# One decode step of a hybrid model: weights loaded from ScalarE's queue, and the recurrence's outer products as matrix products

## The chip, the cores and the metric

The kernel runs on one core of one Trainium2 chip. The metric is the device time of one execution in microseconds; the kernel before took 1142.68 us (median of 3 runs, 1138.63 to 1144.46). A core has five engines that run side by side, each with its own queue of instructions that it works through in order: TensorE (PE in the profile; its weight loads are PEld), VectorE (DVE), ScalarE (ACT), GpSimd (POOL) and SyncE (SP). SP does nothing here but issue DMAs; ACT and POOL issue DMAs too. All DMAs run on the core's 16 DMA engines.

## What is computed

One inference step of one layer for two kinds of tokens at once: a prompt of 512 tokens, and 8 sample requests of one token each with 4096 past tokens. The width is 1024.

```
h  = rmsnorm(x) ; z = h @ w_in              # q, f, v, gate of the recurrence | q, k, v of the attention
S  = f * S + outer(k, v) ; o_hg = q @ S     # gated linear recurrence, 4 heads of 128 x 128
o_da = (softmax(s1) - lam * softmax(s2)) @ v    # differential attention, 4 heads; samples over 32 pages of 128 keys
x  = x + concat(norm(o_hg) * silu(gate), norm(o_da)) @ w_out
x  = x + cross_attention(rmsnorm(x), memory) @ w_mo
x  = x + (silu(h @ w_gate) * (h @ w_up)) @ w_down
```

For the samples the recurrence is one step: the stored state S of each request and head (128 x 128) is scaled by f along its rows and gets the outer product of k and v added; the new state is an output, and q @ S goes on. The samples' attention reads 256 pages of keys and 256 of values, 256 KB each, 134 MB in all; they are the larger part of what is read.

## The kernel before

**Prompt.** Every weight matrix is streamed once. The list `plan` (lines 583 to 608) cuts it into 138 loads of 256 rows by up to 512 columns (512 KB), in the order in which they are used: w_in, the memory's w_mk and w_mv, w_out, w_mq, w_mo, then gate, up and down of the feed-forward part. `load_weights` (613) brings each into a tile `raw`, of which there are three (RAW, later up to six more from the ring `stream`); each load waits until an earlier raw has been used up. ScalarE casts 128 x 512 of it to a rounded `hi` (`round_weights`, 655), VectorE makes the remainder `lo` = raw - hi (`remainders`, 669), with three buffers each (HILO), and `block` (696) makes three products per tile, hi x hi, hi x lo and lo x hi, so that fp32 weights keep their precision; these are the matmuls `mm`.

**Samples.** The same raw tiles are used for the 8 sample rows (`follow`, 2083: sacc, sgm, sgu, sdn). Pages of keys and values come into the ring `stream` (six buffers of two pages) by `gather` (942), issued by SP; `score_keys` (991) multiplies them with the placed queries (`ks`), `sample_softmax` (1024) follows, then `sum_values` (1109, `pv`). Between them stands the prompt's own attention (`da_head`, 1168: sc, pr, pt, oda).

**The samples' recurrence** (`sample_recurrence`, 1474). After the gates, the rows v of all samples (`svq`, 128 x 128: head and sample on the partitions) are written to DRAM (`spill`, 569, the tile `vd`). Then for each of the 8 samples b: GpSimd loads the state `st` and, with `load_row` (575), the four heads' rows of v, copied onto all 128 partitions (`kv`); ScalarE scales each head's part by the column k, `skT[:, h, b]`, which makes the outer product; VectorE adds it to the scaled state, head by head (line 1509); GpSimd stores the state, and TensorE multiplies it with the placed query (`so`).

```
    def load_row(dst, d, b):
        pool.dma_start(dst.rearrange("p (g c) -> p g c", g=4), d[b].partition_broadcast(P))
```

**The order of the work.** Every part is a generator, and `Weave` (312) runs them against a model of the engines' clocks (`Clock`, 134): at each step it takes the stream of the best rank whose data should be there by the model's time of TensorE. What it emits goes to each engine's queue in that order, and the engines run it in order, held by semaphores. A DMA's price in the model stands in `note` (line 248): 0.56 us of the shared issue, and 0.56 us of SP's own time or 0.06 us of ScalarE's. PSUM has 8 banks; the classes mm, at and pv share them (4, 4 and 2 at most).

The weights and the pages are all issued by SP (lines 646 and 952), in one order.

Of the kernel before, what the change touches and what calls it, by code (L numbers as in the profile page):

```python
# [12 lines left out]
F32 = mybir.dt.float32  # L13
# [7 lines left out]
P = 128  # L21
# [4 lines left out]
NB = 8  # L26
# [107 lines left out]
class Clock:  # L134
# [99 lines left out]
    def note(self, e, op, ins):  # L234
        i = ins.ins
        outs = [y.bass_ap for y in i.outs if hasattr(y, "bass_ap")]
        srcs = [y.bass_ap for y in i.ins if hasattr(y, "bass_ap")]
        mine = lambda aps: [a.tensor.name for a in aps if self.tc.is_my_tile(a.tensor)]
        ws, rs = mine(outs), mine(srcs)
        start = self.free[e]  # L240
        at = "dma" if op == "dma_start" else e
        for t in ws + rs:
            w, by = self.wrote.get(t, (0.0, ""))
            if by != at or at == "dma" and t in rs:
                start = max(start, w + self.LATE.get(by, 0.0))
        for t in ws if at != "dma" else ():
            start = max(start, self.used.get(t, 0.0))
        if op == "dma_start":
            if e == "pool":
                self.free[e] = start + 1.0  # L250
            else:
                start = max(start, self.free["issue"])
                self.free["issue"] = start + 0.56
                self.free[e] = start + (0.56 if e == "sp" else 0.06)
            begin = max(self.free["dma"], start + (1.1 if e != "pool" else 2.0))
            a = outs[0] if ws else srcs[0]
            end = self.free["dma"] = begin + 4 * int(np.prod(a.shape)) / 0.37e6
            done = end + 0.93
            e = "dma"
        else:  # L260
            aps = outs + (srcs if e != "pe" else [])
            n = max(int(np.prod(a.shape[1:])) for a in aps)
            holds = self.shared(e, op, outs, srcs)
            if holds:
                for a, b in self.port["pool" if e == "dve" else "dve"]:
                    if a <= start < b:
                        start = b
            done = end = start + self._cost(e, op, outs[0].shape, [a.dtype for a in outs + srcs], n)
            if e == "pe":
                form = "narrow" if outs[0].shape[0] < P else "wide" if F32R in [a.dtype for a in srcs] else "exact"  # L270
                done = end = end + CHANGE.get((self.form, form), 0.0)
                self.form = form
                self.records += 2 if form == "wide" or op == "transpose" else 4
                if self.records >= 256:
                    self.records -= 256
                    done = end = self.fetched = max(end, self.fetched + FETCH)
                tick, rows = int(start / TICK), srcs[0].shape[0] / P
                if self.columns.get(tick - 1, 0) < FULL:
                    done = end = end + (end - start)
                self.columns[tick] = self.columns.get(tick, 0) + n * rows * (1 if F32R in [a.dtype for a in srcs] or op == "transpose" else 2)  # L280
            self.free[e] = end
            self.span = (start, end)
            if holds:
                self.port[e].append((start, end))
        for t in ws:
            self.wrote[t] = (done, e)
            self.mark = max(self.mark, done + self.LATE.get(e, 0.0))
        self.noted += 1
        for t in ws + rs:
            self.used[t] = max(self.used.get(t, 0.0), end)  # L290
            if t in self.banks:
                self.banks[t][1] = self.noted
# [86 lines left out]
def decode_step(ctx: ExitStack, tc: tile.TileContext, io: dict):  # L379
# [186 lines left out]
        use(pt[:, :P].rearrange("p (g b) -> p g b", b=32))  # L566
        at_give()

    def spill(q, name):

        d = dp.tile([P, P], F32, name=name)
        pool.dma_start(d, q)
        return d.rearrange("(g b) c -> b g c", b=32)

    def load_row(dst, d, b):

        pool.dma_start(dst.rearrange("p (g c) -> p g c", g=4), d[b].partition_broadcast(P))


    sizes = [512] * (DFF // 512)  # L580
    sizes.insert(SMALL, DFF % 512)
# [35 lines left out]
    def load_weights():  # L617
        live = deque()

        def home():  # L620

            while live and live[0][0] < min(done["lo"] // 2, done["seen"]):
                live.popleft()
            rings = [t for _, t in live]
            if rings.count("raw") < RAW:
                return "raw", RAW, wp
            if "passed" in S and rings.count("stream") < KBUFS:
                return "stream", KBUFS, kp

        for r, (w, k, c0, ncol, _) in enumerate(plan):  # L630
            yield home
            tag, bufs, pool_ = home()
            live.append((r, tag))
            yield clock.next(tag, bufs)
            raw = ring(pool_, [P, 2, 512], tag, bufs, "raw")[:, :, :ncol]
            src = w[k * P : (k + 2) * P, c0 : c0 + ncol].rearrange("(k p) c -> p k c", p=P)
            if r == 0:
                load_x(0)
                for i in range(2):
                    sync.dma_start(raw[:, i, :], src[:, i, :])  # L640
                load_x(1)
            else:
                if r < 4:
                    load_x(2 * r)
                    load_x(2 * r + 1)
                sync.dma_start(raw, src)
            raws[r] = raw
            if r == CON:
                sync.dma_start(con, io["consts"])
                sync.dma_start(lamv, io["lamv"].partition_broadcast(P))  # L650
                sync.dma_start(ptab, io["ptab"])
            if r == 3:
                sync.dma_start(ropep, io["ropep"])
# [820 lines left out]
    def sample_recurrence(sqT, sfT, svq, sgT):  # L1474
        skT = keep([P, 4, 8], "skT")
        lb3 = lb.unsqueeze(2).to_broadcast([P, 4, 8])
        om3 = omlb.unsqueeze(2).to_broadcast([P, 4, 8])
        sig = rsmall([P, 4, 8], "sig")
        yield from sigmoid(sig, skT, sfT)
        dve.scalar_tensor_tensor(skT, skT, BIG, sig, op0=ALU.min, op1=ALU.mult)  # L1480
        dve.tensor_tensor(skT, skT, om3, op=ALU.mult)
        dve.tensor_tensor(sig, sig, om3, op=ALU.mult)
        dve.tensor_tensor(sfT, sig, lb3, op=ALU.add)
        yield
        sig2 = rsmall([P, 4, 8], "sig")
        yield from sigmoid(sig2, sig2, sgT)
        dve.tensor_mul(sgT, sgT, sig2)
        vd = spill(svq, "vd")
        yield from room(2)
        for b in range(NB):  # L1490
            st = slot("st")
            pool.dma_start(st, io["state"][b])
            kv = slot("kv")
            load_row(kv, vd, b)
            yield
            for h in range(HEADS):
                sl = slice(h * P, (h + 1) * P)
                act.activation(kv[:, sl], kv[:, sl], AF.Copy, scale=skT[:, h, b : b + 1])
            qm = quadt("qm", (P, 4, 32))
            dve.tensor_tensor(  # L1500
                qm,
                sqT[:, :, b : b + 1].to_broadcast([P, 4, 32]),
                ohrow[:, 7 - b : 39 - b].unsqueeze(1).to_broadcast([P, 4, 32]),
                op=ALU.mult,
            )
            yield
            for h in range(HEADS):
                sl = slice(h * P, (h + 1) * P)
                dve.scalar_tensor_tensor(
                    st[:, sl], st[:, sl], sfT[:, h, b : b + 1], kv[:, sl], op0=ALU.mult, op1=ALU.add  # L1510
                )
            yield
            pool.dma_start(io["hg_sample"][b], st)
            yield from at_room()
            po = att("so")
            for h in range(HEADS):
                mm(po[32 * h : 32 * h + 32, :P], qm[:, h, :], st[:, h * P : (h + 1) * P], True, True)
            yield (po,)
            if b == 0:
                dve.tensor_copy(ohg, po[:, :P])  # L1520
            else:
                dve.tensor_add(ohg, ohg, po[:, :P])
            at_give()
        give(2)
        yield
        pool.memset(mixT_s[:, :4, :], 0.0)
        yield from s_headnorm(
            ohg,
            lambda oht: dve.scalar_tensor_tensor(
                mixT_s[:, :4, :8], oht[:, :, :8], hgcol, sgT, op0=ALU.mult, op1=ALU.mult  # L1530
            ),
        )
        S["hgo"] = True
# [1079 lines left out]
```

## Time and profile before

| | |
|---|---|
| median of 3 runs | 1142.68 us (1138.63 to 1144.46) |
| the profiled execution's own time | 1134.85 us |
| its span, first to last instruction | 1133.1 us |
| TensorE busy | 1072.3 us, 95% |
| VectorE, ScalarE, GpSimd busy | 546.1, 428.3, 70.4 us |
| mean granted TensorE clock | 0.974 |
| DMA read, written | 269.35 MB, 8.88 MB |

The profile is that of one execution. Of a group of instructions it gives the busy time, the mean duration in ns, and the idle time of the engine just before them with what ended it. Names are the program's: `ks<-cache_k,qst` writes the tile ks and reads cache_k and qst. Almost all instructions are recorded by one helper and so have one line, L305; go by the names. The ends of matmuls are modelled, so a busy TensorE may hide short waits. fp32 products are recorded as two instructions each, those of rounded operands as one.

### The profile page before, as it was taken

What the parts mean: (1) busy time and instruction counts of PE and PEld (TensorE: products, weight loads), DVE (VectorE), ACT (ScalarE), POOL (GpSimd) and SP (SyncE); (2) the same over time, 40 slices, a digit from 0 to 9 for tenths busy, and PEclk for the clock granted to TensorE, in tenths of its full rate; (3) what the DMA queues carried; (4) which work ended last, traced back from release to release, by engine and by line L of the source; (5) the groups of instructions that cost most, each with busy time, mean ns of one, the idle gap of its engine ahead of it and who ended that gap; (6) DMA issues with size and microseconds to landing.
All of it is one profiled execution on the core that took longest, in us unless ns stands there. A gap on an engine that the chain in (4) does not pass through costs nothing.

```text
span 1133.1 us, 23098 instructions
## 1 busy us (share of the span) xinstructions
PE 1072.3 (95%) x8846; PEld 777.3 (69%) x8846; DVE 546.1 (48%) x1126; ACT 428.3 (38%) x915; POOL 70.4 (6%) x97
## 2 busy tenths in 40 slices
PE   8999799987987889899999999999999999999997
PEld 6777587865665557466666666776577677777776
DVE  6743777534654654444443443453343333443535
ACT  6413443436454556333444332341232221222333
POOL 0000010213101110000300000000000000000002
PEclk9999899988998989999999999999999999999999
DMA  7979665998999995999998799579978982234102
GB/s 255 352 242 324 206 215 174 291 253 259 319 308 278 274 304 169 309 329 332 319 338 285 241 325 343 201 244 359 344 266 291 351 305 75 63 89 129 38 1 75
DMA packets 143376, 279.75 MB, mean 247 GB/s; under 512 B 15281, under 2 KB 20529, under 8 KB 143266
## 3 DMA queue, kind: packets, MB, share of 16 engines
q1 hardware_dynamic: 137970, 264.13, 67.8%
q0 software_dynamic: 4064, 13.05, 6.1%
q8 instruction: 69, 1.13, 0.4%
q10 hardware_dynamic: 1232, 1.11, 0.3%
q14 instruction: 41, 0.34, 0.1%
HBM read 269.35 MB, written 8.88 MB: 246 GB/s over the span
## 4 chain that ended last, share of the span: by engine, by line
PE 81%; DMA 10%; DVE 3%; issue 3%; ACT 1%; SPq 1%; POOL 0%; DVEq 0%; POOLq 0%; ACTq 0%
PE mm L305 56%; DMA cache_k<-cache_k 6%; PE pv L305 5%; PE ks L305 4%; PE sgu L305 2%; PE cs L305 2%; PE sdn L305 1%; DMA kv<-vd 1%; PE ss L305 1%; PE co L305 1%; PE sgm L305 1%; PE pd L305 1%; PE sacc L305 1%; PE oda L305 1%; PE cpv L305 1%
## 5 line engine op out<-in xcount | busy, mean ns | idle before, releaser
L305 DVE TENSOR_TENSOR lo<-raw,hi 128x512 fp32r<-128x512 f32 (+1 forms) x260 | 176.6, 681 | 434.2 <-ACT hi L305 406.1
L305 PE MATMUL mm<-sh,hi 128*128 128x512 f32 (+1 forms) x832 | 339.8, 408 | 4.2 <-ACT sh L305 3.9
L305 ACT CAST hi<-raw 128x512 fp32r<-128x512 f32 (+1 forms) x260 | 157.5, 607 | 490.5 <-PE mm L305 443.3
L305 PE MATMUL mm<-sl,hi 128*128 128x512 f32 (+1 forms) x832 | 324.1, 390 | 0.8 <-DVE sl L305 0.8
L305 PE MATMUL mm<-sh,lo 128*128 128x512 f32 (+1 forms) x832 | 323.0, 388 | 0.0
L305 PEld LDWEIGHTS mm<-sh,hi 128*128 128x128 f32 x832 | 157.2, 189 | 78.6 <-issue 39.0
L305 PEld LDWEIGHTS mm<-sh,lo 128*128 128x128 f32 x832 | 157.5, 189 | 34.0 <-DVE lo L305 0.4
L305 PEld LDWEIGHTS mm<-sl,hi 128*128 128x128 f32 x832 | 157.8, 190 | 28.9 <-DVE sl L305 1.4
L305 PE MATMUL ks<-cache_k,qst 128*32 128x128 f32 x2048 | 72.3, 285 | 16.1 <-DMA cache_k<-cache_k 16.0
L305 PEld LDWEIGHTS ks<-cache_k,qst 128*32 128x32 f32 x2048 | 57.6, 114 | 32.7 <-DMA cache_k<-cache_k 24.0
L305 PE MATMUL pv<-cache_v,wt 128*32 128x512 f32 x512 | 63.4, 608 | 0.0
L305 PE MATMUL mm<-hi,sh 128*128 128x512 f32 x128 | 54.5, 426 | 0.0
L305 PE MATMUL mm<-lo,sh 128*128 128x512 f32 x128 | 50.5, 395 | 0.0
L305 PE MATMUL mm<-hi,sl 128*128 128x512 f32 x128 | 50.5, 394 | 0.0
L305 DVE TENSOR_TENSOR res<-mm,res 128x512 f32<-128x512 f32 (+1 forms) x68 | 42.2, 652 | 9.2 <-PE mm L305 9.2
L305 PEld LDWEIGHTS pv<-cache_v,wt 128*32 128x32 f32 x512 | 14.5, 110 | 31.1 <-issue 22.1
L305 DVE SCALAR_TENSOR_TENSOR lo<-raw,par,hi 128x512 fp32r<-128x512 f32 x16 | 13.2, 826 | 35.1 <-ACT hi L305 35.1
L305 PEld LDWEIGHTS mm<-hi,sh 128*128 128x128 f32 x128 | 24.3, 190 | 7.9 <-issue 3.1
L305 PE MATMUL mm<-hi,mh 128*128 128x512 f32 x64 | 28.5, 446 | 0.9 <-ACT hi L305 0.9
L305 PEld LDWEIGHTS mm<-hi,sl 128*128 128x128 f32 x128 | 24.3, 190 | 5.5
L305 PEld LDWEIGHTS mm<-lo,sh 128*128 128x128 f32 x128 | 24.4, 191 | 4.5 <-issue 0.5
L305 PE MATMUL mm<-lo,mh 128*128 128x512 f32 x64 | 25.2, 394 | 0.2 <-DVE lo L305 0.2
(419 smaller groups left out, 1210.3 us busy)
## 6 DMA issues: line engine op xcount, KB each, us to landing
cache_k<-cache_k SPq DMA_DIRECT2D x256, 256.0 KB, 5.6
cache_v<-cache_v SPq DMA_DIRECT2D x256, 256.0 KB, 4.8
raw<-w_in SPq DMA_DIRECT2D x27, 512.0 KB, 5.1
raw<-w_down SPq DMA_DIRECT2D x22, 512.0 KB, 4.2
raw<-w_gate SPq DMA_DIRECT2D x20, 512.0 KB, 5.0
raw<-w_up SPq DMA_DIRECT2D x20, 512.0 KB, 4.5
cache_mem_k<-cache_mem_k SPq DMA_DIRECT2D x16, 512.0 KB, 6.2
cache_mem_v<-cache_mem_v SPq DMA_DIRECT2D x16, 512.0 KB, 7.4
```

The lines of the kernel that those rows point to most:

```text
L305: ins = getattr(self.engine, op)(*a, **k)
```

## The change

The weights' loads after the fourth (r > CON, CON = 3) are issued by ScalarE instead of SP; SP keeps the pages, the samples' own weights and the first loads. The model's price of a DMA on ScalarE's own time goes from 0.06 to 0.4 us. In the recurrence of the samples the spill to DRAM and the eight broadcast loads go. Instead the rows of v are laid out once, head by head, in a 128 x 512 tile that is zero elsewhere (`vcols`), the columns k are padded and transposed to rows (`krows`), and per sample VectorE keeps of krows the rows of that sample (`km`, a product with a 0/1 column `mine`), and one fp32 matrix product km x vcols gives the four heads' outer products in a PSUM bank (`kv`), from which VectorE updates the state. ScalarE's 32 scalings go.

```diff
@@ -251,7 +251,7 @@
-                self.free[e] = start + (0.56 if e == "sp" else 0.06)
+                self.free[e] = start + (0.56 if e == "sp" else 0.4)
@@ -566,16 +566,6 @@
-    def spill(q, name):
-
-        d = dp.tile([P, P], F32, name=name)
-        pool.dma_start(d, q)
-        return d.rearrange("(g b) c -> b g c", b=32)
-
-    def load_row(dst, d, b):
-
-        pool.dma_start(dst.rearrange("p (g c) -> p g c", g=4), d[b].partition_broadcast(P))
-
@@ -643,7 +633,7 @@
-                sync.dma_start(raw, src)
+                (act if r > CON else sync).dma_start(raw, src)
@@ -1485,17 +1475,25 @@
-        vd = spill(svq, "vd")
         yield from room(2)
+
+        krows, vcols = quadt("krows", tag="rows", bufs=1), slot("vcols")
+        pool.memset(vcols, 0.0)
+        padded, mine = quadt("padded"), rsmall([P, 32], "mine")
+        dve.memset(padded, 0.0)
+        dve.tensor_copy(padded.rearrange("p (h b) -> p h b", h=4)[:, :, :NB], skT)
+        dve.tensor_reduce(mine, ident.rearrange("p (h b) -> p b h", h=4), axis=AX.X, op=ALU.add)
+        yield
+        yield from s_tr(padded, lambda pt: dve.tensor_copy(krows, pt.rearrange("p g b -> p (g b)")))
+        for h in range(HEADS):
+            r = slice(32 * h, 32 * h + 32)
+            act.copy(vcols[r, h * P : (h + 1) * P], svq[r])
+        yield
         for b in range(NB):
             st = slot("st")
             pool.dma_start(st, io["state"][b])
-            kv = slot("kv")
-            load_row(kv, vd, b)
-            yield
-            for h in range(HEADS):
-                sl = slice(h * P, (h + 1) * P)
-                act.activation(kv[:, sl], kv[:, sl], AF.Copy, scale=skT[:, h, b : b + 1])
+            km = quadt("km")
+            dve.tensor_scalar(km, krows, mine[:, b : b + 1], None, op0=ALU.mult)
             qm = quadt("qm", (P, 4, 32))
@@ -1504,11 +1502,16 @@
             yield
+            yield from at_room()
+            kv = att("kv")
+            mm(kv, km, vcols, True, True)
+            yield (kv, st)
             for h in range(HEADS):
                 sl = slice(h * P, (h + 1) * P)
                 dve.scalar_tensor_tensor(
                     st[:, sl], st[:, sl], sfT[:, h, b : b + 1], kv[:, sl], op0=ALU.mult, op1=ALU.add
                 )
+            at_give()
             yield
```

## Rows read from the trace of the kernel before

**Rows 1.** The page, part 1: busy us (share of the span) and instructions by engine

```profile
PE 1072.3 (95%) x8846; PEld 777.3 (69%) x8846; DVE 546.1 (48%) x1126; ACT 428.3 (38%) x915; POOL 70.4 (6%) x97
```

**Rows 2.** Busy time by stretch: length, each engine, granted clock, DMA share, GB/s

```profile
220.00:420.00 200.00, 169.92 (x1702) 121.63 (x1701) 103.12 (x249) 96.74 (x237) 34.15 (x46) 0.92 0.96 281
420.00:620.00 200.00, 195.64 (x1115) 128.59 (x1115) 88.22 (x176) 90.27 (x198) 11.86 (x11) 0.99 0.88 303
620.00:820.00 200.00, 200.00 (x1163) 134.67 (x1162) 83.61 (x153) 61.70 (x108) 1.15 (x3) 1.00 0.83 290
820.00:1080.00 260.00, 259.56 (x1720) 192.82 (x1719) 105.24 (x183) 71.72 (x137) 0.00 (x0) 1.00 0.53 177
```

**Rows 3.** DMA, 220 to 420 us: packets, MB, share; issues, KB, us to landing

```profile
q1 hardware_dynamic: 26015, 47.11, 66.7%
q0 software_dynamic: 2659, 8.72, 29.1%
...
cache_k<-cache_k SPq DMA_DIRECT2D x124, 256.0 KB, 6.9
...
kv<-vd POOLq DMA_DIRECT2D x8, 256.0 KB, 11.4
```

**Rows 4.** The same view, 60 to 200 us

```profile
q0 software_dynamic: 448, 1.31, 2.4%
...
cache_k<-cache_k SPq DMA_DIRECT2D x96, 256.0 KB, 4.8
```

**Rows 5.** Waits of TensorE, 220 to 420 us: us in total, times, longest

```profile
PE ks L305 <- DMA cache_k<-cache_k: 16.0, 10, 6.0
PE sc L305 <- ACT pr L305: 4.9, 1, 4.9
PE so L305 <- issue: 3.6, 1, 3.6
PE pt L305 <- ACT pr L305: 2.3, 1, 2.3
PE mm L305 <- ACT hi L305: 0.9, 1, 0.9
```

**Rows 6.** Timelines of ScalarE, VectorE and TensorE: start, us, instruction, [idle before, releaser]

```profile
232.02 1.28 ACT L305 ACTIVATE kv<-kv,skT 128x128 f32<-128x128 f32 x4 [8.52 <-DMA kv<-vd]
...
234.44 1.13 DVE L305 SCALAR_TENSOR_TENSOR st<-st,scols,kv 128x128 f32<-128x128 f32 x4
...
401.97 1.28 ACT L305 ACTIVATE kv<-kv,skT 128x128 f32<-128x128 f32 x4 [9.32 <-DMA kv<-vd]
...
404.29 2.07 PE L305 MATMUL sc<-kT,qT 64*128 64x512 f32 x2 [4.90 <-ACT pr L305]
```

**Rows 7.** The tile vd: issues (ns min/median/max, first and last start), and who waited

```profile
L305 POOL DMA_DIRECT2D kv<-vd x8: 754/758/762, 222.1 to 388.5; - x8
...
  ACT kv L305: 21.1, 3
```

**Rows 8.** Waits of TensorE's weight loads, 220 to 420 us

```profile
PEld ks L305 <- DMA cache_k<-cache_k: 22.9, 23, 6.3
```

**Rows 9.** Groups of the whole span: busy us, mean ns, idle before

```profile
L305 PE MATMUL ss<-hq,ones 128*128 128x512 f32 x16 | 8.9, 660 | 0.0
...
L305 ACT ACTIVATE kv<-kv,skT 128x128 f32<-128x128 f32 x32 | 10.2, 391 | 21.1 <-DMA kv<-vd 21.1
...
L305 DVE SCALAR_TENSOR_TENSOR st<-st,scols,kv 128x128 f32<-128x128 f32 x32 | 12.2, 443 | 0.0
...
L305 DVE SCALAR_TENSOR_TENSOR S<-S,bhg,pst 128x128 f32<-128x128 f32 x12 | 4.2, 348 | 0.4
...
L305 DVE TENSOR_SCALAR turn<-con,rw 128x128 f32<-128x128 f32 x1 | 0.3, 286 | 0.0
```

**Rows 10.** Issues of the stores of y by ScalarE and SP (ns min/median/max)

```profile
L305 ACTq DMA_DIRECT2D out_y_prompt<-y x4: 378/378/396, 1123.8 to 1129.4; - x4
L305 SPq DMA_DIRECT2D out_y_prompt<-y x4: 372/378/393, 1124.5 to 1128.6; - x4
```

**Rows 11.** Waits of SP's queue, whole span

```profile
SPq L305 <- DVE lo L305: 296.1, 82, 17.4
```

**Rows 12.** Groups of ScalarE, whole span: the casts of the weights

```profile
L305 ACT CAST hi<-raw 128x512 fp32r<-128x512 f32 x244 | 151.0, 620 | 462.9 <-PE mm L305 415.7 <-issue 21.6 <-DMA raw<-w_mk 7.6
```

**Rows 13.** Waits of SP's queue, 220 to 420 us

```profile
SPq L305 <- DVE lo L305: 9.6, 4, 4.3
```

## Prediction

> **What bounds the kernel now.** I read busy time by engine first. TensorE is busy for 1072.3 of 1133.1 us [rows 1], so only what it waits for, or does at a lower clock, can be won; nothing on another engine counts unless TensorE waits for it. Then busy time by stretch: the idle time is in one place. From 220 to 420 us TensorE is busy 169.9 of 200 us, 30.1 us idle, at a mean granted clock of 0.92 (a mix of its two levels, 1.2 and 2.4 GHz); the next 660 us have 4.8 us of idle time in all, at 0.99 to 1.00 [rows 2]. In the same 200 us the DMA engines are busy for 0.96, yet move only 281 GB/s, where the following stretch moves 303 at a share of 0.88 [rows 2]. So the engines are full with something slow.
>
> What it is stands in the DMA view of that stretch. The queue of SP (q1) takes 66.7% of the engines for 47.11 MB: 0.667 x 200 / 47.11 = 2.83 us per MB. GpSimd's queue (q0) takes 29.1%, 58.2 us, for 8.72 MB: 6.7 us per MB [rows 3]. Earlier, from 60 to 200 us, the same q0 needed 0.024 x 140 / 1.31 = 2.56 us per MB [rows 4]; that stretch has no broadcast of v. From 220 to 420 us there are eight: kv<-vd, 256 KB each, 11.4 us to land [rows 3]. With 2.83 us per MB for the other 6.62 MB of q0, 58.2 - 18.7 = 39.5 us are left for the eight, 4.9 us of all 16 engines for each where 256 KB of a page cost 0.74 us. Pages land meanwhile in 6.9 us (median) against 4.8 earlier [rows 3, 4].
>
> Then the waits of TensorE in the stretch: 16.0 us for pages in ks; 4.9 and 2.3 us for ScalarE's pr; 3.6 us in so [rows 5]. The timelines tie the last three to the same loads: ScalarE stands at the broadcast v, 8.52 and 9.32 us at a time, its products kv end, VectorE's st follows at 234.44 us and with it so; TensorE's sc, 4.90 us late at 404.29, waits for a pr that stood behind kv on ScalarE [rows 6]. In total ScalarE waited 21.1 us for kv [rows 7].
>
> **The change part by part.**
>
> *The broadcast goes.* Removed are one spill, eight loads by GpSimd and 32 ScalarE products. Of TensorE's idle time the loads caused 16.0 + 4.9 + 3.6 + 2.3 = 26.8 us [rows 5]. The clock: 0.08 x 169.9 = 13.6 us lost in the stretch [rows 2]; the stretches with few waits have 0.99 and 1.00, so I give back 26.8 / 30.1 of it, 12.1 us; the ends are 0 and 13.6. The weight loads of ks on TensorE waited 22.9 us for pages where its matmuls waited 16.0 [rows 5, 8]; the 6.9 us between lie under modelled ends of matmuls and are worth 0 to 6.9; I take half, 3.4. Together 42.3 us. The DMA side allows no more than 39.5 us, since pages would again be the limit there; so the term is **39.5 us**. What is late next are the pages at the ordinary rate.
>
> ScalarE's 32 products (10.2 us busy [rows 9]) and its 21.1 us of waiting give nothing more: the part that reached TensorE is counted above. GpSimd loses eight issues of 0.76 us [rows 7]; the stores and later loads behind them start sooner, for which TensorE does not wait: 0, covered by stores being outputs.
>
> *The products come to TensorE.* One fp32 product of 128 x 128 by 128 x 512 per sample, eight in all, plus one 128 x 128 transpose. The nearest row is the same shape: ss<-hq,ones, 16 records for 8 products, 8.9 us [rows 9], 1.11 us each. Eight cost 8.9 us, the transpose under 0.3. They stand in a stretch that I have just taken the idle time out of, so all of it is on the path: **-9.2 us** (0 if idle time remains to take it).
>
> VectorE gains eight maskings km (as turn, 0.29 us each [rows 9]), and a few small ones for padded, mine and krows, some 3.5 us; its state update now reads PSUM, as S<-S,bhg,pst does in 0.35 us, no more than the 0.44 us of st now [rows 9]. ScalarE gains four copies to vcols, GpSimd a memset. VectorE is busy 103.1 and ScalarE 96.7 of the 200 us [rows 2]: 0, covered by TensorE's own work; were the cover gone, 5 us. Each kv holds a PSUM bank from the product until its four updates are done; the attention heads draw on the same banks: 0 to 8 x 1.4 = 11 us against (four updates of 0.35), and I take 0, as TensorE has other streams to run in between.
>
> *134 weight loads move to ScalarE* (138 in the plan, the first four stay). One issue on ScalarE takes 0.378 us, like one on SP, which loses them [rows 10]: 51 us in all, on an engine that is idle for 62% of the span [rows 1]: 0 on the path. But ScalarE now also stands at the load until its buffer is free, and behind it are the casts hi, the evacuations and the exponentials; DVE lo, and then the matmuls, wait for hi. SP waited 296.1 us, 82 times, for lo to free such a buffer [rows 11]. ScalarE already stands idle for 462.9 us before its casts, 415.7 of them for matmuls [rows 12], so mostly it would stand there anyway: 0, and the other end is a rival.
>
> *SP keeps pages only.* In the stretch SP stood 9.6 us behind a weight load's buffer [rows 13], pages behind it. If those came sooner for TensorE, up to 9.6 us are won. The Trainium skill speaks against it: "DMA: Bandwidth & Descriptors", section "Issuing engines are not separate DMA queues", says that transfers from several issuing engines run on the same 16 DMA engines and interleave, and that only sequencer time is saved. By that rule this term is 0; by the row alone it is 9.6. I take **3 us**: with a share of 0.96 [rows 2] an earlier issue mostly waits in the queue instead of at SP, and a third is left for the moments in which the queue had run dry. Both ends stay for the range.
>
> *The planner's price* of a load on ScalarE (0.06 to 0.4 us) shifts the order of instructions everywhere; no row shows by how much. Outside 220 to 420 us TensorE is idle for 60.8 - 30.1 = 30.7 us [rows 1, 2]; a different order could win or lose some of it. Ends: a quarter either way, 8 us; taken: 0.
>
> **Sum:** 39.5 - 9.2 + 3 = 33 us. The profiled execution took 1134.85 us and would take 1102. It lies 7.8 us under the median of the runs shown, 1142.68; against that median: **1109 us**.
>
> **The rivals.**
>
> *The pages stay the limit.* Weights and pages now ride in two queues. For: every page wait of the stretch was met with full engines [rows 2, 5]. If a weight load takes engine time from the very page that TensorE waits for, 0.5 MB x 2.83 = 1.5 us are lost at each of the 10 page waits [rows 3, 5], 15 us, and the gain falls to 18: 1124 us. Against: before, the same load stood in front of the page in one queue. A rule of the Trainium skill speaks for this rival: "DMA: Bandwidth & Descriptors", section "Queues, rings and completion order", lets each DMA engine go round between the queues that have work, packet by packet, so a later weight load would overtake pages issued earlier.
>
> *Only the plain page waits go.* The heads' softmax chain (ScalarE, VectorE) keeps TensorE waiting as before, the clock does not come back, and 16.0 - 9.2 = 7 us are won: 1136, with some bank waits 1140, too little to be told from no change.
>
> *Slower: ScalarE held at the weight loads.* Place: the 82 waits for lo [rows 11], now in front of the casts. Price: a cast late by its own 0.62 us [rows 12] each time is 51 us; less the 33 it is +18: 1160 us. It decides from 33 / 82 = 0.40 us of TensorE per wait on. Against: three hi buffers keep the casts ahead, and TensorE waited 0.9 us for hi in the stretch [rows 5].
>
> **How the numbers follow.** The forecast, 1092 to 1120, has 0.67; pages stay the limit 0.17; only page waits 0.06; ScalarE held 0.05; more than forecast (the 9.6 and the order both help), 1085 to 1092, 0.05. A measurement of this kernel can tell about 0.5%, 5.7 us, from no change. Faster: 0.67 + 0.17 + 0.05 = 0.89; same 0.06; slower 0.05. The range of 1086 to 1130 takes in the forecast with the ends of bank, order and split, and most of the first rival.
>
> **What would show it.** Right: no kv<-vd, ScalarE without waits for kv; q0 of that stretch back near 2.6 to 2.8 us per MB; TensorE's waits for cache_k well under 16 us, the stretch with the keys over some 30 us earlier, its clock nearer 0.98; eight new products of about 1.1 us. The 660 us behind it unchanged. Wrong: page waits as long as before with q0 fast (first rival), pr and sc waits as before (second), ScalarE's queue waiting for lo with DVE lo and PE mm late after it (third).

## The result, and the profile after

The change takes 1128.49 us (median of 10 runs, 1119.32 to 1139.74); the kernel before, beside it on the same chip, 1139.97 (10 runs, 1132.16 to 1145.04). The ratio is 0.9899 with a 95% interval of 0.9857 to 0.994: about 11.5 us are won, where 33 were forecast. One of the ten, 1139.74 us, was a slow run; the other nine have a median of 1127.74. The profiled execution took 1124.86 us.

The stretch that the prediction worked on did what it said. Busy time by stretch after the change, with the columns of [rows 2]:

```profile
220.00:420.00 200.00, 197.29 (x1886) 142.75 (x1885) 121.21 (x302) 111.60 (x260) 29.17 (x41) 1.00 0.86 300
420.00:620.00 200.00, 192.66 (x1008) 120.42 (x1007) 78.13 (x142) 73.82 (x158) 10.16 (x9) 0.97 0.80 271
620.00:820.00 200.00, 199.35 (x1169) 132.07 (x1171) 81.95 (x153) 60.53 (x105) 1.16 (x3) 1.00 0.83 295
820.00:1080.00 260.00, 260.00 (x1692) 195.68 (x1692) 105.62 (x183) 72.12 (x136) 0.00 (x0) 1.00 0.48 162
```

The columns are the length of the stretch, the busy time of TensorE, of its weight loads, of VectorE, ScalarE and GpSimd, the granted clock, the DMA share and GB/s. From 220 to 420 us TensorE is idle for 2.7 us instead of 30.1, its granted clock is 1.00 instead of 0.92, and the DMA engines move more at a lower share. In the next 200 us it is the other way round: 7.3 us idle instead of 4.4, the clock 0.97 instead of 0.99, the DMA share down from 0.88 to 0.80 and the rate from 303 to 271 GB/s. Less busy DMA engines in a stretch that reads pages, while TensorE is idle longer, are the mark to follow up: they suggest that loads are issued too late, which the rows below bear out.

DMA from 220 to 420 us (q10 is ScalarE's queue, which now carries the weights), beside [rows 3]:

```profile
q1 hardware_dynamic: 21490, 38.19, 54.8%
q10 hardware_dynamic: 6819, 13.15, 19.1%
q0 software_dynamic: 2530, 8.25, 11.1%
...
cache_k<-cache_k SPq DMA_DIRECT2D x118, 256.0 KB, 5.6
```

GpSimd's queue q0 takes 0.111 x 200 / 8.25 = 2.69 us per MB, where it took 6.7. TensorE's waits in the stretch, beside [rows 5]; the waits for ScalarE's pr, in sc and in so, are gone from them:

```profile
PE ks L305 <- DMA cache_k<-cache_k: 1.2, 5, 0.3
PE pt L305 <- DVE pr L305: 0.8, 1, 0.8
PE mm L305 <- DVE lo L305: 0.4, 2, 0.2
PE mm L305 <- ACT hi L305: 0.2, 1, 0.2
```

Groups of the whole span, beside [rows 9, 12]:

```profile
L305 PE MATMUL kv<-vcols,km 128*128 128x512 f32 x16 | 8.4, 605 | 0.0
...
L305 DVE SCALAR_TENSOR_TENSOR st<-st,scols,kv 128x128 f32<-128x128 f32 x32 | 9.0, 341 | 4.1 <-PE kv L305 4.1
...
L305 ACT CAST hi<-raw 128x512 fp32r<-128x512 f32 x244 | 151.1, 620 | 472.2 <-PE mm L305 439.7 <-DMA raw<-w_in 9.9 <-DMA cache_mem_k<-cache_mem_k 7.7
```

The eight products cost 8.4 us of TensorE, and VectorE's update takes 341 ns on average instead of 443, no more than before, as costed. The last matmul of the keys (ks) starts at 375.9 us, 42.9 us earlier than before (418.8). But the values' matmuls (pv) then run from 411.0 to 695.2 us, 284 us, where they ran from 446.7 to 703.6, 257 us: 27 of the 43 us are lost there. What SP's queue stands for from 420 to 620 us, the kind of wait as in [rows 11, 13] (us in total, times, longest):

```profile
SPq L305 <- PE pv L305: 32.0, 13, 6.5
SPq L305 <- DMA raw<-w_mq: 26.6, 7, 6.1
SPq L305 <- DMA raw<-w_mo: 11.9, 3, 5.2
SPq L305 <- DMA raw<-w_out: 9.8, 3, 6.0
```

SP issues none of these weights any more, and yet waits 48.3 us, 13 times, for weights (raw) to land. Before, it stood for VectorE's lo there:

```profile
SPq L305 <- DVE lo L305: 34.4, 14, 9.9
```

The chain of waits around one of them, in order of time (start us, us, what):

```profile
458.37 0.63 ACT hi L305
459.02 0.70 DVE lo L305
459.75 7.25 DMA raw<-w_mq
...
467.12 0.33 SPq L305
...
468.21 4.82 DMA cache_v<-cache_v
...
473.07 1.71 PE pv L305 x4
```

VectorE's lo frees a weight buffer; ScalarE, which stood there for it, issues the load at 459.75; it lands at 467.00; only then does SP issue the next page, 0.12 us later, and TensorE's pv waits for it. In the trace's records every load signals a semaphore as it lands, and SP's and ScalarE's loads signal the same eight (numbers 101 and 103 to 109) in turn. Before each load the issuing engine waits on that load's semaphore, so that a page whose turn falls on one waits until the load that had it before has landed; in the chain above the weight load and the page behind it both have number 105. GpSimd's loads use eight others. What that does shows where TensorE takes a page in as its operand (PEld), waits from 420 to 620 us:

```profile
PEld pv L305 <- DMA cache_v<-cache_v: 19.6, 23, 2.8
```

Before the change that row had 6.4 us:

```profile
PEld pv L305 <- DMA cache_v<-cache_v: 6.4, 18, 0.7
```

### The profile page after: what moved, and what is told of

Same layout as the page of the kernel before. It is cut to its first block, busy times and chain, and to the rows that moved or that the text cites. A ratio compares the mean times of both kernels' runs of the same rounds, so it can differ in the third digit from the quotient of the medians.

```text
span 1123.1 us, 23051 instructions
## 1 busy us (share of the span) xinstructions
PE 1079.7 (96%) x8863; PEld 776.1 (69%) x8863; DVE 549.6 (49%) x1140; ACT 421.8 (38%) x887; POOL 63.2 (6%) x89
## 4 chain that ended last, share of the span: by engine, by line
PE 82%; DMA 8%; DVE 5%; ACT 2%; issue 2%; SPq 1%; DVEq 0%; ACTq 0%
PE mm L305 58%; PE pv L305 5%; PE ks L305 4%; DMA raw<-w_in 2%; PE sgu L305 2%; DMA cache_v<-cache_v 2%; PE cs L305 2%; PE sdn L305 1%; DMA cache_k<-cache_k 1%; PE sgm L305 1%; DVE lo L305 1%; PE co L305 1%; DMA raw<-w_mq 1%; PE ss L305 1%; ACT hi L305 1%
## 5 line engine op out<-in xcount | busy, mean ns | idle before, releaser
L305 DVE TENSOR_TENSOR lo<-raw,hi 128x512 fp32r<-128x512 f32 (+1 forms) x260 | 179.7, 693 | 424.9 <-ACT hi L305 380.4
L305 PE MATMUL pv<-cache_v,wt 128*32 128x512 f32 x512 | 75.1, 608 | 5.5 <-DMA cache_v<-cache_v 5.3
L305 PE MATMUL ks<-cache_k,qst 128*32 128x128 f32 x2048 | 66.3, 279 | 1.2 <-DMA cache_k<-cache_k 1.2
L305 PEld LDWEIGHTS pv<-cache_v,wt 128*32 128x32 f32 x512 | 15.6, 109 | 47.6 <-issue 26.2
L305 ACT ACTIVATE hi<-raw,par 128x512 fp32r<-128x512 f32 x16 | 11.6, 724 | 42.3 <-PE mm L305 33.8
```

The lines of the kernel that those rows point to most:

```text
L305: ins = getattr(self.engine, op)(*a, **k)
```

## The experiments

The theory (theory 1) was that the broadcast's 39.5 us came back in full, and were lost again because SP waits for ScalarE's loads to land. Of the sixteen kernels, the first four take the change apart.

**1. Products only, weights on SP.**

```diff
-                (act if r > CON else sync).dma_start(raw, src)
+                sync.dma_start(raw, src)
-                self.free[e] = start + (0.56 if e == "sp" else 0.4)
+                self.free[e] = start + (0.56 if e == "sp" else 0.06)
```

> Only the recurrence's part of the change: outer products on TensorE, no broadcast loads; weights stay on SP's queue with the old price. Theory 1 (the 39.5 us of the broadcast loads came back in full, but with the weights on ScalarE's queue SP now stands for landings of weight loads, 48.3 us of waits on raw in 420 to 620 us, and the values' pages come late): some 30 us under before, about 1110 us, and no wait of SP's queue for the landing of a weight load. Theory 2 (the values' stretch loses what the keys' stretch wins, whichever queue the weights are in, since its limit is the pages' rate): as the change, about 1128 us. Theory 3 (the products cost much more than 9.2 us): also about 1128, but with waits around kv in the stretch 220 to 420 us.

Measured: 1106.6 us, ratio 0.972 (0.969 to 0.9751), 34 us under the kernel before. The products are worth what the prediction gave to the whole change. Theories 2 and 3 fall.

**2. Queue only.** The broadcast loads stay, the weights go to ScalarE.

```diff
-                sync.dma_start(raw, src)
+                (act if r > CON else sync).dma_start(raw, src)
-                self.free[e] = start + (0.56 if e == "sp" else 0.06)
+                self.free[e] = start + (0.56 if e == "sp" else 0.4)
```

> Only the queue's part: the broadcast loads and ScalarE's products are kept as before, the 134 weight loads go to ScalarE's queue, with the new price. Theory 1: slower than before by some 10 to 20 us (1150 to 1160), with SP's queue waiting for landings of weight loads between 420 and 620 us. Theory 2: the split is worth nothing by itself, within 5 us of before. A third outcome, faster than before by 5 us or more, would say that the prediction's +3 us had the right sign.

Measured: 1175.2 us, ratio 1.0323 (1.0288 to 1.0359), 34 us slower, more than the theory gave. The prediction's +3 us had the wrong sign, unless the order of this kernel, which shifts with the price, is what costs; the runs with a fixed order below decide that.

**3 and 4. Weights on GpSimd; the old price.**

```diff
-                (act if r > CON else sync).dma_start(raw, src)
+                (pool if r > CON else sync).dma_start(raw, src)
```

> The changed kernel with the 134 weight loads issued by GpSimd instead of ScalarE. SP still keeps pages only. Theory 1: in the change SP's and ScalarE's loads share eight completion semaphores and wait for each other's landings; GpSimd's use eight others, so SP's waits for the landing of weight loads (140.3 us on raw for w_up alone in the change) vanish, and the values' stretch gets its pages in time: about 1110 us, unless GpSimd itself comes late with weights, which would show as waits of DVE hi or ACT hi for raw and of TensorE for hi. Theory 2 (a split of weights and pages over two queues is what costs, by sharing the DMA engines): as the change, about 1128 us.

> The changed kernel with the planner's old price of a DMA on ScalarE (0.06 us in place of 0.4), so only the order of instructions differs. Theory 1: within 5 us of the change (1123 to 1134), SP's waits for landings of weight loads still there. Rival (the order that the new price makes is what cost the missing 20 us): about 1108 us, 20 us under the change.

Measured: 1105.9 us (0.9696; 0.9667 to 0.9725) with GpSimd, without a wait of SP for raw; 1135.8 us (0.9962; 0.9934 to 0.9991) with the price alone put back as in the second pair of lines of experiment 1. So the price is not what costs; it is worth 7 us as the change has it. The first is near theory 1's 1110; the second lies 2 us outside the 1123 to 1134 that theory 1 gave it, on the side away from its rival. But each of these kernels also has an order of its own, since the planner prices the issuer. The next runs therefore hold the order of all other instructions fixed: the load is issued by one engine and entered in the plan as another's.

**5, 9, 10, 13. One order, the change's, and four ways to issue.** In 10 SP issues, in 9 GpSimd. In 5 and 13 ScalarE also writes one column of the buffer first, so that it stands where the change makes it stand; GpSimd (5) or SP (13) then issues the load. The diff of 13; the others leave out the copy or put `pool` for `sync`:

```diff
-                (act if r > CON else sync).dma_start(raw, src)
+                if r > CON:
+                    act.engine.copy(raw[:, 0, :1], ident[:, :1])
+                    act.clock.note("act", "dma_start", sync.engine.dma_start(raw, src))
+                else:
+                    sync.dma_start(raw, src)
```

> The changed kernel, instruction for instruction in the same order on every engine, except that each of the 134 weight loads is issued by GpSimd, and ScalarE writes one column of the load's buffer in its place, which the load then overwrites. So ScalarE stands still at the same places and for the same buffers as in the change, but no DMA of ScalarE shares semaphores with SP's. Theory 1 (SP held until ScalarE's weight loads have landed): the loss goes, about 1107 us. Rival (ScalarE standing at the loads, with its casts and evacuations behind it, is what costs, the third rival of the prediction): about 1128 us, as the change. A value half way would divide the loss between the two.

> The changed kernel, every engine's other instructions in the same order, with the 134 weight loads issued by GpSimd: the fifth experiment without ScalarE's stand-in, so neither SP nor ScalarE stands for a weight. If ScalarE's standing is what kept the fifth at 1121 us, this one is at about 1106 us. If the order that the change's planner writes out is what costs there, it stays at 1116 to 1122 us.

> The changed kernel in its own order of instructions on TensorE, VectorE and ScalarE, but with the weight loads issued by SP, as before the change. Theory 1 (SP held for the landing of ScalarE's loads is the larger part of the loss): some 10 to 15 us under the change, 1113 to 1119 us, more where the order costs nothing. Rival (the order alone, at whatever queue): within 4 us of the change, about 1128 us.

> The tenth experiment (the change in its own order, weights issued by SP, 1098.7 us), where ScalarE in addition writes one column of each weight's buffer at the place at which the change has ScalarE issue the load; SP's load then follows it. ScalarE stands as in the change, and its loads are not in its queue. Theory 1 (SP held for landings costs): 1097 to 1104 us. Rival (ScalarE's standing costs): 1115 to 1128 us.

**11 and 12. The order of the first experiment,** issued by ScalarE and by GpSimd (the same edit on experiment 1, entered in the plan as SP's).

> The first experiment (products only, 1106.6 us) with all engines' other instructions in its own order, but the 134 weight loads issued by ScalarE. It sets the queue alone against 1106.6 us, with no change of order. Theory 1: 15 to 30 us more, 1122 to 1137 us (the low-price run, with ScalarE issuing in another order, had 1135.8). Rival (the loss came with the order): 1104 to 1112 us.

> The first experiment in its own order, with the 134 weight loads issued by GpSimd: SP keeps pages only and neither SP nor ScalarE stands for a weight. It measures by itself what the prediction priced at +3 us (0 to 9.6): 1097 to 1107 us. Theory 1 says that it is at or under 1106.6 us; a rival by which two queues that take turns cost pages their engine time has it 10 us or more above.

Measured, median us (ratio to before, interval):

| issued by | change's order | order of experiment 1 |
|---|---|---|
| SP | 1098.7 (0.9645; 0.9616 to 0.9674) | 1106.6 (0.972; 0.969 to 0.9751) |
| SP, ScalarE stands too | 1104.3 (0.9659; 0.9628 to 0.9689) | |
| GpSimd | 1115.3 (0.9793; 0.9763 to 0.9822) | 1125.7 (0.9879; 0.9847 to 0.991) |
| GpSimd, ScalarE stands too | 1121.4 (0.9823; 0.9778 to 0.9868) | |
| ScalarE | 1128.5 (the change) | 1132.8 (0.9957; 0.9923 to 0.999) |

Down a column only the issuer differs, and whether ScalarE stands. ScalarE's queue costs 1128.5 - 1098.7 = 29.8 us in the one order and 26.2 in the other. ScalarE's standing is 5.6 us of it with SP issuing and 6.1 with GpSimd; by the ratios to the kernel before, which was run beside each, 1.6 and 3.4. So 24 to 28 us are left for the queue itself. Across a row is the order: the change's is 4 to 10 us better, so that run 10 came out 14 us under what theory 1 gave it, and run 9's second reading, that this order costs, falls with it.

The GpSimd rows were a surprise: the fifth and twelfth runs missed what theory 1 expected, and the twelfth has the time that its rival gave, two queues that take engine time from the pages. SP waits for no weight there, and still it is 17 to 19 us slower than SP issuing. But the values' pages come in time: TensorE's weight loads of pv wait for them 8.5 us in the whole span in run 9, 8.6 in run 10 and 20.6 in the change; 12.1 in run 12, 14.7 in experiment 1 and 30.3 in run 11. So a second queue alone, here GpSimd's, does not make them late, and GpSimd brings a cost of its own. Timelines of run 9, VectorE and then GpSimd:

```profile
554.10 0.69 DVE L305 TENSOR_TENSOR lo<-raw,hi 128x512 fp32r<-128x512 f32 x1 [3.20 <-ACT hi L305]
...
556.82 9.51 DVE L305 TENSOR_TENSOR lo<-raw,hi 128x512 fp32r<-128x512 f32 x1 [0.82 <-ACT hi L305]
```

```profile
555.09 0.72 POOL L637 DMA_DIRECT2D raw<-w_mo  x1 [12.61 <-DVE lo L305]
555.84 9.94 POOL L305 TENSOR_TENSOR res<-sh,sl 128x512 f32<-128x512 f32 x8
```

GpSimd stood 12.61 us at a weight load, its eight sums came behind it, and a lo of 0.69 us took 9.51 beside them; TensorE's cs then waits 4.5 and 2.6 us for VectorE. Another part is early: TensorE's sacc, which reads raw itself, waits 8.5 us for it up to 220 us in run 9 and 1.0 in run 10. By sum these waits are some 15 of the 17 us by which run 9 is slower. So GpSimd is no clean stand-in, and the agreement of run 3 with theory 1 was partly its order; why that order escapes the cost, with a VectorE subtraction of 10.25 us of its own at 544 us, stays open.

The chain from 440 to 600 us sets the change against run 10, whose order is the same (shares by line); first the change, then run 10:

```profile
by line: PE mm L305 41.1%; PE pv L305 18.1%; DMA cache_v<-cache_v 11.9%; DMA raw<-w_mq 7.6%; PE cs L305 7.5%; PE co L305 4.6%; PE cpt L305 1.7%; ACT cp L305 1.6%; DVE lo L305 1.3%; ACT hi L305 1.2%; SPq L305 1.2%; issue 0.8%; DVE cmx L305 0
```

```profile
by line: PE mm L305 58.6%; PE pv L305 20.2%; PE cs L305 7.5%; PE co L305 7.2%; PE cpt L305 1.7%; ACT cp L305 1.6%; PE po L305 0.7%; PE ss L305 0.5%; DVE cmx L305 0.5%; DVE lo L305 0.4%; ACT hi L305 0.4%; ACT cph L305 0.3%; DVE cpl L305 0.3%
```

Loads, some 20% of the chain in the change, are not in it in run 10; the values' matmuls there run from 407.2 to 670.9 us.

**6. Where it sits.** Experiment 1 with the 24 loads of w_out, w_mq and w_mo on ScalarE, the others on SP.

```diff
-                sync.dma_start(raw, src)
+                (act if any(w is io[n] for n in ("w_out", "w_mq", "w_mo")) else sync).dma_start(raw, src)
```

> The first experiment (products only, all weights on SP, 1106.6 us) with the 24 loads of w_out, w_mq and w_mo alone moved to ScalarE; they fall in the stretch in which the values' pages are read. Theory 1: the loss sits where weight loads and pages alternate, so these 24 of 134 bring much more than their share: 10 to 20 us, 1117 to 1127 us. Rival (the loss is spread evenly over the 134 loads, 0.17 us each): 4 us, about 1111 us.

Measured: 1122.2 us (0.9833; 0.9786 to 0.988), 15.6 us more than experiment 1. By the ratios it is 13 us. The order shifts a little with this edit, since the plan has these loads as ScalarE's. So these 24 of 134 loads bring about half of the 26 us, much more than their share: the loss sits largely where weight loads alternate with the values' pages. Where the other half sits is not shown.

**14. Waits for landings, without ScalarE.** On run 10; `spot` is one number in memory.

```diff
+                    if any(w is io[n] for n in ("w_out", "w_mq", "w_mo")):
+                        sync.engine.dma_start(spot, raw[:1, 0, :1])
```

> The tenth experiment (1098.7 us), where SP after each of the 24 loads of w_out, w_mq and w_mo also copies one number of the loaded buffer to a spare place in memory, so that SP stands until the load has landed, some 5.3 us each, before it issues the next page. ScalarE is as in the tenth. Theory 1: the values' pages come late and TensorE's pv waits for them, 10 to 35 us more, 1109 to 1134 us. Rival: within 4 us of 1098.7, since SP stood there for VectorE's lo anyway.

Measured: 1147.3 us (1.0057; 1.0032 to 1.0082), 48.6 us more than run 10, beyond the range given. SP's waits from 420 to 620 us, and those of TensorE's weight loads:

```profile
SPq L641 <- DMA raw<-w_mq: 42.8, 8, 6.9
SPq L641 <- DMA raw<-w_mo: 31.4, 6, 6.5
SPq L641 <- DMA raw<-w_out: 11.6, 2, 6.6
```

```profile
PEld pv L305 <- DMA cache_v<-cache_v: 50.8, 50, 2.8
```

With ScalarE out of it, the same mechanism gives the same signature, stronger: the values' pages come late. All 24 landings hold SP for 117 us in the span. A loss per us of standing can't be carried over from that to the change, since SP also stands in run 10, for lo, from 420 to 620 us:

```profile
SPq L637 <- DVE lo L305: 30.7, 15, 5.0
```

What TensorE pays can be read directly: the busy time of pv, whose modelled ends hide part of the waiting, and the idle time before it, in runs 10, 13, 9, the change and this run:

```profile
L305 PE MATMUL pv<-cache_v,wt 128*32 128x512 f32 x512 | 62.5, 598 | 0.0
L305 PE MATMUL pv<-cache_v,wt 128*32 128x512 f32 x512 | 62.3, 599 | 0.0
L305 PE MATMUL pv<-cache_v,wt 128*32 128x512 f32 x512 | 63.4, 599 | 0.0
L305 PE MATMUL pv<-cache_v,wt 128*32 128x512 f32 x512 | 75.1, 608 | 5.5 <-DMA cache_v<-cache_v 5.3
L305 PE MATMUL pv<-cache_v,wt 128*32 128x512 f32 x512 | 95.8, 601 | 16.6 <-DMA cache_v<-cache_v 16.4
```

Where SP issues the weights, with or without ScalarE standing, and where GpSimd does, pv takes 62 to 63 us. In the change it takes 18.1 us more, of the 26.4 us between the profiled executions of the change and of run 10 (spans 1123.1 and 1096.7). In this run it takes 49.9 us more, which accounts for the whole 48.6. Experiment 13 and this one take the two parts separately. The granted clock from 420 to 620 us, 0.97 in the change and 1.00 in run 10, is worth up to 0.03 x 192.7 = 5.8 us more (an estimate); the rest of the 26.4 is near what ScalarE's standing costs.

**15 and 16. Later issue.** Each load later in the program, on ScalarE (the change) and on SP (run 10).

```diff
-            while live and live[0][0] < min(done["lo"] // 2, done["seen"]):
+            while live and live[0][0] < min((done["lo"] - 2) // 2, done["seen"]):
```

> The changed kernel, with each weight load put one row of weights later into the program (after two more lo), so that its buffer is free when ScalarE gets there. The order of the instructions shifts with it. Theory 1: SP's waits for landings of weight loads in 420 to 620 us (48.3 us) fall to under 20, and the time to 1100 to 1115 us, unless the weights then come too late, which would show as hi waiting for raw. Rival (it is the sharing of the engines by two queues that costs, or the order): 1124 to 1132 us.

> The same later place with the weights on SP's queue (the tenth experiment, 1098.7 us, with the shift). SP then hardly stands for lo (34 us in 420 to 620 us of the kernel before). If pages held behind weights still cost anything there, it gains up to 9.6 us, 1090 to 1098 us; if not, 1097 to 1103 us; if weights come too late, more.

Measured: 1119.2 us (0.9805; 0.977 to 0.9841) on ScalarE, above what theory 1 expected. The reason stands in SP's waits from 420 to 620 us of that run:

```profile
SPq L305 <- DMA raw<-w_mq: 18.8, 6, 5.3
SPq L305 <- DMA raw<-w_mo: 12.2, 2, 6.5
SPq L305 <- DMA raw<-w_out: 10.4, 3, 4.7
```

They are 41.4 us, not under 20: the edit did not remove what it was to remove, and the run tells little more than that most of the loss stays where the waits stay. Where its 9 us come from, the shifted order or fewer waits, is not shown. On SP it is 1096.0 us (0.9571; 0.9541 to 0.9601), the fastest of all, 32 us under the change and 45 under the kernel before. All five of its runs (1090.45 to 1096.44) lie below all six of run 10 (1096.74 to 1099.34): it gains 2.6 us by the medians, 8 by the ratios, inside the 1090 to 1098 expected if pages held behind weights still cost something. SP's waits for lo from 420 to 620 us fall from 30.7 to 9.1 us. The order shifts too, and the two are not told apart.

**7 and 8. The two terms of the products.** A plain load in place of the broadcast, in the kernel before; and each product made twice, in experiment 1.

```diff
-            load_row(kv, vd, b)
+            pool.dma_start(kv, io["state"][b])
```

```diff
             mm(kv, km, vcols, True, True)
+            mm(kv, km, vcols, True, True)
```

> The kernel before with each broadcast load of v replaced by a plain load of the same 256 KB (the sample's state, so the outer product is made of the wrong rows and the sample's new state is not the reference's); the same number of issues, bytes and ScalarE products. Theory 1 (the broadcast's access pattern costs 39.5 us of the engines, its bytes 8 x 0.74 us): about 1103 us, the queue q0 near 2.6 to 2.8 us per MB from 220 to 420 us. Rival (the loads cost by being eight more loads that ScalarE waits for, whatever their pattern): within 10 us of before.

> The first experiment with each of the eight outer products made twice into the same bank. As the prediction has it, all of a product lies on the path: 8 x 1.11 = 8.9 us more, 1115 to 1116 us. Rival (the products are hidden in idle time that the stretch keeps): 0 to 3 us more, 1107 to 1110 us.

Measured for 7: 1098.1 us (0.9624; 0.9567 to 0.968), 43 us less, by the interval 37 to 50. DMA from 220 to 420 us in that run:

```profile
q0 software_dynamic: 3181, 10.40, 13.9%
...
kv<-state POOLq DMA_DIRECT2D x7, 256.0 KB, 6.6
```

With as many loads of the same bytes the queue now takes 0.139 x 200 / 10.40 = 2.67 us per MB: the cost was the broadcast's pattern. In the records a broadcast load writes four pieces of 512 B to each partition, the same for all, and a plain one a single piece of 2048 B; the run does not tell the small pieces from the shared source. For 8: 1110.9 us (0.973; 0.9686 to 0.9774), 4.3 us more than experiment 1 by the medians, between the two expectations, and 1 by the ratios, as its rival has it; the intervals do not tell 0 from 9.

## Why the prediction was wrong, point by point

- **What bounds the kernel** was right: with the eight broadcasts went the waits for ScalarE's pr and in so, and of the 16.0 us for the keys' pages 1.2 are left.
- **39.5 us for the broadcast:** 43 us by experiment 7 (37 to 50). The size is right. The cap that gave it, the pages as the next limit, was not met: the DMA share of that stretch fell to 0.86.
- **-9.2 us for the products:** they have 8.4 us of busy time and lie between 0 and 9 us on the path (experiment 8); experiment 1, 34 us, holds both terms, whose sum was 30.3.
- **Planner's price, 0 between -8 and +8:** +7 us (experiment 4: 1135.8 against 1128.5). Within its ends, near the far one. The whole order of the change, with the issuer entered in the plan, is worth 4 to 10 us against that of experiment 1.
- **"SP keeps pages only", +3 us between 0 and 9.6:** this is the step that failed, in its sign. The move of the weights as a whole costs 29.8 us at a fixed order (26.2 in the other); 1.6 to 5.6 of that are ScalarE's standing, which the step before it (**"134 weight loads move to ScalarE"**) had at 0, and 24 to 28 fall on this step. The measured steps, 34 for the products, 8 for the order and -30 for the queue, lead from the kernel before to the change by way of experiments 1 and 10 and so come to about the measured 11.5 by construction; they divide the difference and prove nothing more.

How it failed: the step asked what SP would no longer stand behind, and took the end of that wait for free pages. It did not ask what else a page's issue waits for. With the weights in its own queue, SP stood for lo and issued the load and the next pages one after the other. With them on ScalarE, ScalarE stands for lo and issues the load, and the page that shares the load's semaphore waits for the landing on top: 13 waits of 3.7 us on average from 420 to 620 us, 6.1 at the longest; the landing itself took 7.25 us in the chain above. Pages held up behind a weight load were not set free; SP's 30.7 us of standing for lo (run 10) became 48.3 us of standing for landings. That the standing for lo cost something is likely, by run 16, which cuts it on SP's own queue and gains 2.6 to 8 us. So the wait that the step wanted to remove was there, and the move did not remove it. "The 660 us behind it unchanged" fell with it, and the step was priced in the stretch with the keys, where the loss is not; it is in the stretch with the values, which the prediction had read as nearly free of idle time and looked at no further.

The Trainium skill's rule on this step ("DMA: Bandwidth & Descriptors", "Issuing engines are not separate DMA queues"), that transfers from several issuing engines run on the same 16 DMA engines and only sequencer time is saved, would have made the term 0. That is nearer than the 3 us, and the runs do not agree with that 0 either: at a fixed order the weights on ScalarE's queue cost 26 to 30 us.

- **The rivals.** "The pages stay the limit" gave 1124 us, near the measured time, by another way: more engine time for weights, full engines. The trace has page waits of 1.2 us in the keys' stretch and idle engines (0.80) in the values'. "Only the plain page waits go" fell: the waits for ScalarE's pr are gone, and the clock came back to 1.00. "ScalarE held at the weight loads" was the right place to look and a small part: 1.6 to 5.6 us by run 13, where 51 were priced.
- **What would show it** named page waits in the keys' stretch and "the 660 us behind it unchanged", which was the sign that failed; the rows which decide, SP's waits for raw, were not on the list.

Open: what makes up the part of the 24 to 28 us that does not stand at pv; and whether ScalarE could carry the weights if its loads shared no semaphore with SP's. That was not tried.

## What to carry to other kernels

Before loads are moved to another engine's queue to free the first, look at what the first engine's issues wait for: if both signal the same few semaphores in turn, a load held on one stops the other until it has landed, and the wait to be removed comes back longer. A row "SPq <- DMA x" for an x that SP does not load is the sign. And when one change has two parts, the part priced at "about nothing" deserves both signs in its range: here the products alone, with the weights left where they were and the new order kept, took 1098.7 us.

## What the runs showed of the hardware

- SP's and ScalarE's loads in this program signal eight semaphores in common, and SP stood 48.3 us for ScalarE's landings in 200 us.
- A 256 KB load that copies four rows of 512 B to all 128 partitions cost about 43 / 8 = 5.4 us of this kernel's time more than a plain load of the same size, whose pieces are 2048 B.
- A VectorE subtraction of 0.69 us took 9.51 us beside 9.94 us of GpSimd sums. The Trainium skill ("SBUF — State Buffer", "SBUF: two separate sides") says that a VectorE operation with two SBUF inputs and a GpSimd operation that reads SBUF share a port pair, and whichever starts first holds it for its whole instruction. Run 9 shows a longer wait: the subtraction ends at 566.33 us, after the last of the eight sums (565.78), where one sum takes 1.24 us. In run 10 a subtraction beside the same sums took 1.65 us instead of 0.75. So both happen, and no run shows what decides.
